# Recurrence of an RWKV-7 / SGU trunk: where three kinds of tiles lie

## The chip, the cores and the metric

The kernel runs on one core of a Trainium2 chip. A core has a matrix engine (TensorE, PE in the profile), a vector engine (DVE), a scalar engine (ACT), a general engine (POOL) and a sync engine (SP) that issues DMAs. Each engine works through its own list of instructions in order; waits between engines are semaphores. The metric is the device time of one execution in microseconds (us), the median over the runs.

## The reference

Two layers over one sequence of 512 tokens of width 1024. Layer 0 is RWKV-7 time mixing, layer 1 a spatial gating unit (SGU); each is followed by a SwiGLU feed-forward block (FFN), and every sub-layer stands between two RMS norms. The change lies in layer 0, whose core is, for each of 16 heads of 64 features:

```python
xx = _token_shift(x) - x
xs = x[None] + xx[None] * mix[:, None, None, :]
r, k, v = jnp.einsum('cbtd,cde->cbte', xs[:3], w_rkv)
...
S = (S * w_t[:, :, None, :]
     + sa[..., None] * b_t[:, :, None, :]
     + v_t[..., None] * k_t[:, :, None, :])
y = jnp.einsum('bhij,bhj->bhi', S, r_t)
...
y = y + jnp.sum(r_h * k_h * r_k, axis=-1, keepdims=True) * v_h
return (y * g) @ w_o
```

Here sa is S times a_t. Each head's y is normalised over its 64 features before the bonus term is added.

## The kernel before

The recurrence is done in chunks of 64 tokens, 8 chunks, for four batches of four heads (b = 0 to 3). The list PLAN fixes the order in which the stages are written: P (r and k projections), E (decay and key features, early stage), X0 (the inputs of the value projection), V0 to V3 (value projection), F (front: within-chunk matrices), B (back: inverts the 64-step triangular systems and builds each chunk's transition), S (the scan over chunks), N (group norm, bonus, gate). After N3 comes the output projection with w_o, then FFN 0, the SGU layer and FFN 1. The list is not the order of execution: a scheduler takes all instructions of all five engines and puts them in order by priorities and by when it expects a tile's buffer to be free. So which pool a tile lives in decides which instruction has to wait for which earlier tile, and that moves instructions on every engine.

The steps that the prediction speaks of, by name and line:

- X0: `mixed_split` makes eight tiles `xsp`, one for each block kt of 128 features. Each is made from `xs` by ACT (L612) and DVE (L613), then split in a high part (ACT cast, L179) and a low part (DVE, L180). The value projection `v_proj` multiplies them, twelve matmuls for each kt, kt 0 first, so a late `xsp` stops the PE. String XV names the pool of each: x for the residual's pool, e for the early stage's, s for the general slots.
- E3, the last early stage, shares the engines with X0: `ssp` (PE, L785), its Relu (ACT, L787), a table load and logarithm (L788), a table load and exponential (L789).
- F: groups of four matmuls `lm` (L851), copied by ACT into `MV`, `LA` and `BX`, masked by POOL; transposes `bkt` (L865). `BX` holds, for each half of the chunks and of the heads, what later extends the matrices (`gh`, L966).
- B: DVE transposes `LA` into `LX` (L882), inverts in 15 steps of two operations (`tm` L896, `Dm` L898), transposes the result twice (`hn` L901, `Dt` L902). PE and DVE then pass `Qp`, `Qs` (L921), `Np`, `Tp`, `Q2p`, `T2p`, `mp` and eight `gh` to each other, and DVE adds each `gh` into `MV` (L968, L969).
- S: for each chunk `us` (PE, L995), `su` (DVE, L997), `Yp` (PE); the result is copied into `Y` by ACT (L1010).
- N: `mu` (L1024), centring (L1026), variance `va` (L1030), a root by Newton steps (L214 to L223), `vt` transposes of the bonus (L1045, after `hn`, L1042, and before ACT's `ob`, L1047), `yt` (L1070, L1071), gate (L1074, L1075).

The pools: the residual's pool xp has 4 buffers of 128 x 1024 floats and is idle in the recurrence, apart from the tiles that borrow it; the early stage's pool, tag e2, has E2 = 7; the general slots, tag s, 17. Helpers `s4`, `xslot` and `e2` take a tile from the general slots, the residual's pool and the early stage's pool. `front` also takes its `ST` and `LA`, and `back` its `LX`, from e2.

Of the kernel before, what the change touches and what calls it, by code (L numbers as in the profile page):

```python
# [7 lines left out]
F32 = mybir.dt.float32  # L8
# [5 lines left out]
P = 128  # L14
# [3 lines left out]
TT = T // P  # L18
H2 = 8
C = 64  # L20
# [12 lines left out]
SLOTS = 17  # L33
E2 = 7
PLAN = "P0 E0 P1 E1 P2 E2 P3 E3 X0 F0 B0 F1 V0 V1 V2 V3 B1 S0 F2 S1 F3 N0 B2 N1 B3 S2 N2 S3 N3".split()
XV = "xxxessss"
XSLOTS = 13
LAG = 2
PLAIN = 2
# [91 lines left out]
class Trunk:  # L131
# [384 lines left out]
    def rwkv(self, x0):  # L516
# [3 lines left out]
        with ExitStack() as ctx:  # L520
# [14 lines left out]
            def e2(name, shape=(P, 2, T), dt=F32):  # L535
                return rp.tile(list(shape), dt, name=name, tag="e2", bufs=E2)

            def s4(name, shape, dt=F32):
                return self.slot(shape, dt, name)

            def xslot(name, shape, dt=F32):
                return self.xp.tile(shape, dt, name=name, tag="x", bufs=TT)
# [73 lines left out]
            def mixed_split(c, where):  # L616
                r = []
                for kt in range(KT):
                    t = mixed(c, kt)
                    new = dict(x=xslot, s=s4, e=e2)[where[kt]]  # L620
                    s = new("xsp", [P, 2, T], F32R)
                    self.split(s[:, 0, :], s[:, 1, :], t)
                    r.append(s)
                return r
# [192 lines left out]
            def upper(t, base):  # L817

                g.affine_select(out=t, in_=t, compare_op=ALU.is_ge, fill=0.0, base=base, pattern=[[0, 4], [1, C]],
                                channel_multiplier=-1)  # L820
# [3 lines left out]
            def front(b, o):  # L824

                MV, ST, BX = {}, {}, {}
# [14 lines left out]
                for hh, q in units:  # L841
                    st, mv = ST[hh][:, q], MV[hh, q]

                    bx = BX[hh, q] = s4("BX", [P, 4, 4, C])
                    for hd in range(2):
                        g.tensor_copy(bx[head[hd], 2 + hd], self.ident[head[hd], head[hd]].unsqueeze(1).broadcast_to([64, 4, C]))
                    for hd in range(2):
                        rows, other = head[hd], head[1 - hd]
                        lm = self.bank("pl", "lm")
                        for cc in range(4):  # L850
                            mm(lm[:, cc * P:(cc + 1) * P], st[:, cc].rearrange("p n t -> p (n t)"), mv[:, cc, :, hd, :], start=True, stop=True)  # L851
                        lv = lm.rearrange("p (c a t) -> p c a t", c=4, a=2)
                        la = LA[:, q, 4 * hh:4 * hh + 4]
                        a.copy(mv[other, :, :, hd], lv[other])
                        for n in range(2):
                            upper(mv[other, :, n, hd], n - 1)
                        a.copy(la[rows], lv[rows, :, 0, :])
                        upper(la[rows], -1)
                        a.copy(bx[rows, 1], lv[rows, :, 1, :])
                        upper(bx[rows, 1], 0)  # L860

                    sf = st.rearrange("p c n t -> p c (n t)")
                    pt = self.bank("pl", "bkt")
                    for cc in range(4):
                        nc.tensor.transpose(pt[:, cc * P:(cc + 1) * P], sf[:, cc], self.ident)  # L865
                    pv = pt.rearrange("p (c h f) -> p c h f", c=4, h=2)
                    for hd in range(2):
                        rows, other = head[hd], head[1 - hd]
                        a.copy(bx[rows, 0], pv[rows, :, hd])
                        a.copy(bx[other, 2 + hd], pv[other, :, hd])  # L870
# [100 lines left out]
            def scan(b, o, then=None):  # L971

                MV, pc = o["MV"], o["pc"]
                Y = xslot("Y", [P, TT, 2, P])

                def new_su(c):
                    su = rp.tile([P, 2, 2, C], F32, name="su", tag="su", bufs=4)
# [8 lines left out]
                for c in range(NC):  # L986
                    hh, cc = c // 4, c % 4
# [21 lines left out]
                    if par == 1:  # L1009
                        a.copy(Y[:, tt].rearrange("p q f -> p (q f)"), yp[:, 0:2 * P])  # L1010
                    if c < NC - 1:
                        su = nsu
                    if then and c == NC // 2 - 1:
                        then(Y)
                return Y

            def group_norm(Y, tts):

                n, n4 = len(tts), 4 * len(tts)
                ts = slice(tts[0], tts[-1] + 1)  # L1020
                y4 = Y[:, ts].rearrange("p t q (h v) -> p (t q h) v", h=2)
                yf = Y[:, ts].rearrange("p t q f -> p (t q f)")
                mu = self.sm.tile([P, n4], F32, name="mu", tag="mu", bufs=2)
# [71 lines left out]
            xr, kr, ops, Y = None, {}, {}, {}  # L1095
            for n in PLAN:
                f, b = n[0], int(n[1])
# [6 lines left out]
                elif f == "X":  # L1104
                    xs = mixed_split(2, XV)
                elif f == "V":
# [164 lines left out]
```

## Time and profile before

| | |
|---|---|
| time, median of 3 runs | 1363.42 us (1361.05 to 1363.58) |
| profiled execution | 1364.19 us, span 1362.5 us |
| mean granted PE clock | 0.975 |
| PE busy | 1289.8 us, 95% of the span, 9812 matmuls |
| DVE busy | 894.2 us, 66% |
| ACT busy | 694.9 us, 51% |
| POOL busy | 193.2 us, 14% |

Times below are in us from the start of the span. In the tables of stretches each engine has its busy time and its number of instructions, and PEclk is the clock granted to the PE as a share of full speed. In the lists of waits, an engine and line is followed by what it waited for, the total, how often and the longest. In the timelines a row has start, duration, engine, line, operation, and in brackets the idle time before it and what ended that.

Three stretches of the recurrence matter here: the value projection, 172 to 252, with the fronts F0 and F1 and the back B0 around it; the scans and backs, 252 to 401; and the end of the recurrence with the output projection, up to 473.

### The profile page before, as it was taken

The numbers are of one execution on the slowest core, as the hardware profiler recorded it, in microseconds if no ns is written. First come the engines' busy times: TensorE is split into PE (matmuls) and PEld (weight loads), VectorE is DVE, ScalarE is ACT, GpSimd is POOL, SyncE is SP. The second block draws the span as 40 slices with busy tenths as digits, with TensorE's granted clock in tenths as the row PEclk, the third lists the DMA queues.
The fourth block names the chain that finished last, engine by engine and source line by source line (L and its number), as shares of the span: only waits on it lengthen the run. The fifth ranks groups of instructions, "written<-read, shape, count | busy, mean of one in ns | idle before, by whom it ended". The sixth has DMA issues, their size and how long they took to land. (4 is left out here: it accounts for less than half of the span.)

```text
span 1362.5 us, 24563 instructions
## 1 busy us (share of the span) xinstructions
PE 1289.8 (95%) x9812; PEld 1120.0 (82%) x9812; DVE 894.2 (66%) x1515; ACT 694.9 (51%) x1240; POOL 193.2 (14%) x311
## 2 busy tenths in 40 slices
PE   5989999989789989999999999999989999999998
PEld 3657789878677787999998887878878999998886
DVE  7875676477837499778785325575479787786223
ACT  7975795576333364455454314543364554464221
POOL 1000184575100024000000002010122000000000
PEclk9989999899799988999999999999989999999999
DMA  5136595322214233343323232242322433323321
GB/s 157 38 89 154 138 221 162 108 73 78 78 42 153 63 105 90 112 117 100 106 78 109 93 116 86 79 151 80 108 82 72 126 109 94 109 63 117 99 94 62
DMA packets 217266, 140.10 MB, mean 103 GB/s; under 512 B 67856, under 2 KB 193344, under 8 KB 217152
## 3 DMA queue, kind: packets, MB, share of 16 engines
q1 hardware_dynamic: 215856, 133.81, 34.0%
q0 software_dynamic: 1296, 4.72, 1.0%
q8 instruction: 77, 1.26, 0.4%
q14 instruction: 37, 0.30, 0.1%
HBM read 124.35 MB, written 14.16 MB: 102 GB/s over the span
## 5 line engine op out<-in xcount | busy, mean ns | idle before, releaser
L180 DVE TENSOR_TENSOR wlo<-wraw,whi 128x1024 fp32r<-128x1024 f32 x105 | 129.6, 1234 | 195.2 <-ACT whi L179 187.4
L179 ACT CAST whi<-wraw 128x1024 fp32r<-128x1024 f32 x105 | 110.0, 1048 | 227.9 <-PE acc L204 136.5
L204 PE MATMUL acc<-whi,actw 128*128 128x512 f32 x704 | 220.7, 394 | 0.0
L204 PEld LDWEIGHTS acc<-whi,actw 128*128 128x128 f32 x704 | 132.3, 188 | 30.6
L204 PE MATMUL Q<-bc,whi 128*128 128x256 f32 x864 | 156.3, 281 | 1.1 <-ACT hn L421 1.1
L204 PE MATMUL acc<-wlo,actw 128*128 128x512 f32 x352 | 138.7, 394 | 0.0
L204 PEld LDWEIGHTS Q<-bc,whi 128*128 128x128 f32 x864 | 133.4, 189 | 1.5 <-ACT hn L421 1.3
L179 ACT CAST whi<-wsum 128x1024 fp32r<-128x1024 f32 x72 | 75.5, 1051 | 101.1 <-DVE wsum L377 35.5
L204 PE MATMUL Q<-bc,wlo 128*128 128x256 f32 x432 | 121.5, 281 | 0.0
L204 PE MATMUL Z<-bc,whi 128*128 128x256 f32 x576 | 107.9, 285 | 3.3 <-ACT whi L179 3.3
L204 PE MATMUL R<-bc,whi 128*128 128x256 f32 x576 | 108.1, 285 | 0.9 <-ACT Q L392 0.9
L180 DVE TENSOR_TENSOR wlo<-wsum,whi 128x1024 fp32r<-128x1024 f32 x72 | 86.7, 1221 | 18.9 <-ACT whi L179 18.9
L204 PE MATMUL gu<-hT,whi 128*128 128x256 f32 (+1 forms) x384 | 92.2, 334 | 3.6 <-DVE hT L62 3.4
L204 PEld LDWEIGHTS Z<-bc,whi 128*128 128x128 f32 x576 | 90.6, 192 | 4.2 <-ACT whi L179 4.2
L204 PEld LDWEIGHTS R<-bc,whi 128*128 128x128 f32 x576 | 91.0, 192 | 1.3 <-ACT Q L392 1.1
L204 PE MATMUL proj<-xsp,whi 128*128 128x512 f32 x256 | 85.2, 411 | 5.7 <-ACT xsp L179 3.1
L179 ACT CAST whi<-wq 128x1024 fp32r<-128x1024 f32 x54 | 56.7, 1049 | 58.1 <-issue 18.4
L180 DVE TENSOR_TENSOR wlo<-wq,whi 128x1024 fp32r<-128x1024 f32 x54 | 65.9, 1222 | 30.9 <-ACT whi L179 30.8
L204 PE MATMUL Z<-bc,wlo 128*128 128x256 f32 x288 | 81.9, 284 | 0.0
L204 PE MATMUL R<-bc,wlo 128*128 128x256 f32 x288 | 81.9, 284 | 0.0
L204 PEld LDWEIGHTS Q<-bc,wlo 128*128 128x128 f32 x432 | 81.9, 189 | 0.0
L204 PEld LDWEIGHTS acc<-wlo,actw 128*128 128x128 f32 x352 | 66.1, 188 | 15.3
(346 smaller groups left out, 2883.3 us busy)
## 6 DMA issues: line engine op xcount, KB each, us to landing
wraw<-in_ffn_w_down_dram SPq DMA_DIRECT2D x44, 512.0 KB, 3.7
wq<-in_ffn_w_gate_dram SPq DMA_DIRECT2D x72, 256.0 KB, 3.0
wq<-in_ffn_w_up_dram SPq DMA_DIRECT2D x72, 256.0 KB, 3.5
wraw<-in_rwkv_w_rkv_dram SPq DMA_DIRECT2D x24, 512.0 KB, 4.9
wraw<-in_sgu_w_in_dram SPq DMA_DIRECT2D x16, 512.0 KB, 4.2
x<-in_x_dram SPq DMA_DIRECT2D x8, 512.0 KB, 4.2
ST<-sb SPq DMA_DIRECT2D x8, 512.0 KB, 6.2
MV<-sa SPq DMA_DIRECT2D x32, 128.0 KB, 3.8
```

What stands on the lines that cost most here:

```text
L179: self.nc.scalar.copy(hi, src)
L180: self.nc.vector.tensor_tensor(lo, src, hi.bitcast(F32), op=ALU.subtract)
L204: self.nc.tensor.matmul(out, l, r, start=start, stop=stop, skip_group_check=resumed)
```

## The change

Three places take their tiles elsewhere. The eight inputs of the value projection came from the residual's pool (kt 0 to 2), e2 (kt 3) and the general slots (kt 4 to 7); now kt 0 and 1 come from e2 and the other six from the general slots. The `BX` tiles of the even batches (F0 and F2, four tiles each) came from the general slots and now come from the residual's pool. The scan's result `Y` came from the residual's pool and now comes from e2. No size of a pool changes and no arithmetic.

```diff
-XV = "xxxessss"
+XV = "eessssss"
...
-                    bx = BX[hh, q] = s4("BX", [P, 4, 4, C])
+                    bx = BX[hh, q] = (s4 if b % 2 else xslot)("BX", [P, 4, 4, C], F32)
...
-                Y = xslot("Y", [P, TT, 2, P])
+                Y = e2("Y", (P, TT, 2, P))
```

All five engines' lists come out in another order. Two places carry the prediction. The first is ACT at the start of the value projection, where the last tiles `xsp` are cast while E3 finishes. Before:

```order
L179 CAST xsp<-xs 128x512
L772 ACTIVATE cum<-cum,lnh 128x1024
L787 ACTIVATE tws<-ssp,tiny 128x512
L179 CAST xsp<-xs 128x512
L777 ACTIVATE kp<-tws,hka 128x512
L787 ACTIVATE tws<-ssp,tiny 128x512
L179 CAST whi<-wraw 128x1024
L788 ACT_TABLE_LOAD
L788 ACTIVATE tws<-tws,tiny 128x1024
```

And after:

```order
L772 ACTIVATE cum<-cum,lnh 128x1024
L787 ACTIVATE tws<-ssp,tiny 128x512 x2
L612 ACTIVATE xs<-h,omix 128x512
L179 CAST xsp<-xs 128x512
L788 ACT_TABLE_LOAD
L788 ACTIVATE tws<-tws,tiny 128x1024
L179 CAST xsp<-xs 128x512
L789 ACT_TABLE_LOAD
```

Before, both casts (kt 6 and kt 7) stood ahead of the second Relu of E3 (L787). Now the cast for kt 6 stands behind both Relus and behind the making of kt 7's `xs`, and the cast for kt 7 behind the table load and the logarithm as well. On the PE the two `ssp` products that the Relus read moved in the same way: before, 18 and 27 value products stood behind the first and the second; now both stand together behind 60 value products, with 34 of the 36 products with kt 5, 6 and 7 right behind them.

The second place is DVE at the third inversion (batch 2), around `LX`. Before:

```order
L222 SCALAR_TENSOR_TENSOR nr_t<-nr_t,nr_a 128x16
L882 STREAM_TRANSPOSE LX<-LA 128x1024
L223 SCALAR_TENSOR_TENSOR nr_y<-nr_t,nr_y 128x16
L896 TENSOR_TENSOR tm<-LX,Dm 128x2x15
L221 TENSOR_TENSOR nr_t<-nr_y 128x16
L898 TENSOR_TENSOR Dm<-Dm,tm 128x2x15
L222 SCALAR_TENSOR_TENSOR nr_t<-nr_t,nr_a 128x16
L896 TENSOR_TENSOR tm<-LX,Dm 128x2x28
L223 SCALAR_TENSOR_TENSOR nr_y<-nr_t,nr_y 128x16
L968 TENSOR_TENSOR MV<-gh,BX 128x4x64
```

And after:

```order
L968 TENSOR_TENSOR MV<-gh,BX 128x4x64
L969 TENSOR_TENSOR MV<-gh,MV 128x4x64
L1075 TENSOR_TENSOR ob<-gate,ob 128x512
L997 TENSOR_TENSOR su<-us,pc 64x2x64
L1071 SCALAR_TENSOR_TENSOR ob<-yt,vecT_101,ob 128x512
L997 TENSOR_TENSOR su<-us,pc 64x2x64
L882 STREAM_TRANSPOSE LX<-LA 128x1024
L896 TENSOR_TENSOR tm<-LX,Dm 128x2x15
L898 TENSOR_TENSOR Dm<-Dm,tm 128x2x15
L1075 TENSOR_TENSOR ob<-gate,ob 128x512
```

Before, `LX` of batch 2 stood inside the Newton steps of N0, ahead of the first of batch 1's eight pairs of additions into `MV` (L968, L969). Now it stands behind the last of these pairs and behind four of the seven `su` of scan S1.

The third place is DVE at the end of that inversion. Before, batch 2's `Qs` (L921) and the fourth inversion's `LX` stood thus:

```order
L902 STREAM_TRANSPOSE Dt<-Dm 128x32x32
L997 TENSOR_TENSOR su<-us,pc 64x2x64
L180 TENSOR_TENSOR g2l<-g_4827,g2h 128x256
L997 TENSOR_TENSOR su<-us,pc 64x2x64 x2
L921 TENSOR_TENSOR Qs<-Qp,id_144 128x512
L1024 TENSOR_REDUCE mu<-Y 128x16
L882 STREAM_TRANSPOSE LX<-LA 128x1024
L180 TENSOR_TENSOR wlo<-wraw,whi 128x1024
L1025 TENSOR_SCALAR mu<-mu 128x16
L896 TENSOR_TENSOR tm<-LX,Dm 128x2x15
L1026 TENSOR_TENSOR Y<-Y,mu 128x1024
```

And after:

```order
L1026 TENSOR_TENSOR Y<-Y,mu 128x1024
L898 TENSOR_TENSOR Dm<-Dm,tm 128x2x15
L901 STREAM_TRANSPOSE hn<-Dm 128x32x32
L902 STREAM_TRANSPOSE Dt<-Dm 128x32x32
L882 STREAM_TRANSPOSE LX<-LA 128x1024
L1030 TENSOR_REDUCE va<-hn 128x16
L896 TENSOR_TENSOR tm<-LX,Dm 128x2x15
L214 TENSOR_SCALAR nr_a<-va 128x16
L898 TENSOR_TENSOR Dm<-Dm,tm 128x2x15
L216 TENSOR_SCALAR nr_h<-nr_a 128x16
L921 TENSOR_TENSOR Qs<-Qp,id_144 128x512
```

The mean and the centring of N1 (L1024 to L1026), which stood behind `Qs`, now stand ahead of the transposes of batch 2's inverse; `LX` of batch 3 and N1's variance (L1030) stand ahead of `Qs`. Three low splits of w_o's weights (`wlo`, L180), which stood between `Qs` and batch 3's transposes, have left this stretch for a place behind batch 3's inversion.

Three more moves matter. On the PE, all of F1's `lm` and `bkt` and B0's first `mp` now stand ahead of the last value product (before, two `lm` groups and two `bkt` of F1 and that `mp` stood behind it). Between the end of S1 and batch 2's first `gh` the PE's list now holds F3's last four `lm` and two `bkt` and the steps of B2, and little else. At the end, the first half of N3 (`vt`, `yt`, gate) stands inside S3, before behind its last `Yp`.

## The prediction

> **What bounds the kernel now.** I read the page first, for the busiest engine and for where it is not busy.
>
> ```profile
> PE 1289.8 (95%) x9812; PEld 1120.0 (82%) x9812; DVE 894.2 (66%) x1515; ACT 694.9 (51%) x1240; POOL 193.2 (14%) x311
> PE   5989999989789989999999999999989999999998
> ```
>
> The PE is the bound of the program as a whole. A slice of the second row is 34 us: from the 17th on (545 us, FFN 0 and later) it is a row of nines. What follows the recurrence is thus a solid chain of PE work that the change leaves alone, and a microsecond gained or lost before it reaches the end undiminished. So only the recurrence counts. I took it in stretches of 20 us; the PE has its busy time behind the stretch's length, and PEclk follows behind POOL.
>
> ```profile
> 180.00:200.00 20.00, 17.41 (x171) 16.91 (x169) 14.15 (x13) 17.89 (x34) 14.53 (x20) 1.00 0.98 212
> 340.00:360.00 20.00, 12.59 (x241) 10.40 (x240) 17.91 (x53) 9.38 (x14) 4.52 (x8) 0.70 0.25 80
> 440.00:460.00 20.00, 17.73 (x75) 13.86 (x76) 7.79 (x18) 3.93 (x7) 0.00 (x0) 0.91 0.33 103
> 460.00:480.00 20.00, 16.03 (x80) 12.36 (x79) 12.99 (x43) 11.96 (x35) 3.37 (x2) 1.00 0.27 80
> ```
>
> The value projection (180 to 200) is nearly full. The worst stretch is 340 to 360, where the PE idles 7.4 us and DVE is busy 17.91 of 20: there DVE's inversion of batch 3 is the bound. The end (440 to 480) idles 2.27 + 3.97 = 6.2 us. The lists of the PE's waits say what ended the idle time, first for 165 to 255, then 252 to 400, then 400 to 500.
>
> ```profile
> PE lm L851 <- DMA MV<-sa: 1.5, 1, 1.5
> PE lm L851 <- POOL MV L819: 1.1, 1, 1.1
> ...
> PE vt L1045 <- DVE hn L1042: 3.8, 1, 3.8
> ...
> PE vt L1045 <- ACT ob L1047: 1.3, 1, 1.3
> PE yt L1070 <- ACT ob L1047: 0.8, 1, 0.8
> ```
>
> No wait is for a buffer in so many words: a pool shows itself in which instruction stands where. So I go by the order of the lists, and price what moved with rows of the trace.
>
> **Part one: the inputs of the value projection.** On the PE, the value products run at a fixed pace, and the two `ssp` come among them. ACT and DVE rows of the same moment stand below.
>
> ```profile
> 177.23 1.02 PE L785 MATMUL ssp<-tws,bones 128*128 128x512 f32 x2
> 179.03 0.40 PE L204 MATMUL v<-whi,xsp 128*128 128x256 f32 x2
> 180.80 0.40 PE L204 MATMUL v<-whi,xsp 128*128 128x256 f32 x2
> ...
> 176.23 0.71 ACT L612 ACTIVATE xs<-h,omix 128x512 f32<-128x512 f32 x1
> 179.86 0.61 ACT L179 CAST xsp<-xs 128x512 fp32r<-128x512 f32 x1
> 181.08 0.68 ACT L787 ACTIVATE tws<-ssp,tiny 128x512 f32<-128x512 f32 x1
> 182.71 1.28 ACT L788 ACT_TABLE_LOAD   x1
> 184.00 1.15 ACT L788 ACTIVATE tws<-tws,tiny 128x1024 f32<-128x1024 f32 x1
> ...
> 180.50 0.69 DVE L180 TENSOR_TENSOR xsp<-xs,xsp 128x512 fp32r<-128x512 f32 x1 [1.43 <-ACT xsp L179]
> ```
>
> Between the two value rows lie 15 products in 1.77 us, 0.118 each. Before, the last `xsp` was split by 180.50 + 0.69 = 181.2, well ahead of its use. With the change, 60 products stand ahead of both `ssp`. If they begin near 172.4, the `ssp` begin at 172.4 + 60 x 0.118 = 179.5 and end at 180.5. The two Relus (0.68 each) then end near 181.6, kt 7's `xs` (0.71) at 182.3, the cast for kt 6 (0.61) at 182.9, the table load at 184.2, the logarithm at 185.3, the cast for kt 7 at 185.9, and its split (0.69) at 186.6. The PE has worked through kt 5 and 6 (24 products, 2.8 us) at 183.4 at the earliest. It waits for kt 7 until 186.6: 3.2 us of new idle time, split over kt 6 and kt 7. In return, the two waits for `MV` in the list above (1.5 and 1.1) fall away, since the DMA and POOL work they wait for lands while the PE stands: net **+0.6**. Bounds: 0, if ACT reaches the Relus earlier, since kt 7 then arrives earlier too; +4.9, if the 2.6 are not won back and the PE restarts at a lower clock. That last has a row: in 340 to 360, where the 3.8 us wait lies, the granted clock was 0.70; the lost 0.30 on the next 48 products (5.7 us) is 1.7.
>
> [...]
>
> **Part two: `BX` in the residual's pool, F1 and F3.** The general slots that F0's `BX` no longer holds go to F1, whose last two `lm` groups and `bkt` come ahead of the end of the value projection. That is work moved on a full PE, not removed: S0 begins later by that work, and has that much less of it between its own steps. I take **0**. Bounds: it could win the 1.1 us of the second wait quoted above, if that copy is the one that now comes early, or lose as much, if the longer stretch before S0 is not made up behind it.
>
> **Part three: the two inversions on DVE.** This is the largest move. Rows of DVE, before:
>
> ```profile
> 301.10 1.96 DVE L882 STREAM_TRANSPOSE LX<-LA 128x1024 f32<-128x1024 f32 x1
> 304.13 0.42 DVE L968 TENSOR_TENSOR MV<-gh,BX 128x256 f32<-128x256 f32 x1
> 317.23 0.41 DVE L969 TENSOR_TENSOR MV<-gh,MV 128x256 f32<-128x256 f32 x1
> 324.68 1.92 DVE L902 STREAM_TRANSPOSE Dt<-Dm 128x1024 f32<-128x1024 f32 x1
> 334.53 0.69 DVE L921 TENSOR_TENSOR Qs<-Qp,id 128x512 f32<-128x512 f32 x1 [0.16 <-PE Qp L918]
> 366.68 0.38 DVE L968 TENSOR_TENSOR MV<-gh,BX 128x256 f32<-128x256 f32 x1
> ...
> L898 DVE TENSOR_TENSOR Dm<-Dm,tm 128x30 f32<-128x30 f32 (+7 forms) x30 | 8.2, 274 | 0.4
> L896 DVE TENSOR_TENSOR tm<-LX,Dm 128x30 f32<-128x30 f32 (+7 forms) x30 | 8.1, 269 | 0.4
> L180 DVE TENSOR_TENSOR wlo<-wraw,whi 128x1024 fp32r<-128x1024 f32 x3 | 3.6, 1208 | 0.9 <-ACT whi L179 0.9
> L1026 DVE TENSOR_TENSOR Y<-Y,mu 128x1024 f32<-128x1024 f32 x1 | 1.2, 1224 | 0.0
> L1024 DVE TENSOR_REDUCE mu<-Y 128x16 f32<-128x1024 f32 x1 | 1.2, 1220 | 1.3 <-ACT Y L1010 1.3
> L1025 DVE TENSOR_SCALAR mu<-mu 128x16 f32<-128x16 f32 x1 | 0.5, 474 | 0.0
> L1075 DVE TENSOR_TENSOR ob<-gate,ob 128x512 f32<-128x512 f32 x3 | 2.1, 692 | 1.0 <-PE gate L1074 0.9
> ```
>
> (The lower rows are groups over 298 to 367; both inversions lie in it, so one has half of 8.2 + 8.1.)
>
> The additions of batch 1 come first now: without `LX` and the first steps ahead they may begin some 2.7 us earlier, 301.4, and run at their pace of before (304.13 to 317.64, 13.5 us) to 314.9; with 0.6 from part one, 315.5. One `ob` (0.7) later `LX` of batch 2 starts, near 316.5, where it had started at 301.10. It ends at 318.5. The 30 operations take 8.2 us. Among them now stand an `ob` and two splits of `oT` of its size (2.1 together), mean, scaling and centring of N1 (1.2 + 0.5 + 1.2), and three `su` and two small weight pieces that I put at 2: 7 in all. The last `su` also has to wait for the scan, which I put at 2 more. That makes 318.5 + 8.2 + 7 + 2 = 335.7, two transposes like `Dt` (1.92 each) 339.5, `LX` of batch 3 (as the other, 1.96), the variance (a reduction of the mean's size, 1.2) and small steps (1) 343.7, so near 344 for `Qs`, against 334.53: **nine us later**.
>
> From `Qs` to the first addition of batch 2 it took 366.68 - 334.53 = 32.15 before, DVE busy in most of it. Of what DVE did there, these are now done elsewhere: `LX` 1.96, mean 1.2, its scaling 0.5 and the 1.3 of waiting ahead of it, centring 1.2, variance 1.2, three `wlo` 3.6: 11.0. That leaves 21.2, so the additions start at 344 + 21.2 = 365.2. Against 366.68 that is **-1.4**: nearly all that `LX` lost, the shorter list behind `Qs` gives back. Bounds: -3.4 if the `su` do not hold DVE up; +2.5 if both inversions run 2 us slower, with more waits.
>
> The PE needs time for the same chain, so I checked it: in batch 3, `Qs` to the first `gh` (L966) took
>
> ```profile
> 381.33 0.68 DVE L921 TENSOR_TENSOR Qs<-Qp,id 128x512 f32<-128x512 f32 x1
> 400.88 1.37 PE L966 MATMUL gh<-BX,MVt 64*128 64x128 f32 x13
> ```
>
> 19.6 us, with scan work between. From 344 that is 363.6, before DVE's 365.2; DVE still decides. From there on, batch 3's own chain repeats the same steps, shifted.
>
> **Part four: `Y` in e2, and the end.** With half of N3's transposes inside S3, the waits for `ob` in the third list (1.3 + 0.8) are covered by the scan's chain. Behind the last `Yp` there are then fewer transposes and about as many output products, so what `ob` no longer delays may wait for the second half's `ob` instead. I take half of the 2.1, **-1.1**; bounds -2.1, all of it, and +1, if the moved transposes hold up S3's own steps by about one of the waits quoted.
>
> **The sum**: +0.6 is already within the 315.5 and so in the -1.4; 0 - 1.4 - 1.1 = -2.5. The profiled execution took 1364.19, the median is 1363.42, 0.8 lower. From the median: 1363.4 - 2.5 = **1360.9**, 1361 us. About 0.2%, 2.7 us, is what a measurement here can tell from no change, so my forecast lies just inside that. All the lower bounds together are -3.4 - 1.1 - 2.1 = -6.6, all the upper ones, without the +4.9 that has a case of its own, 2.5 + 1.1 + 1 = +4.6: its own range is 1357 to 1368.
>
> **Rivals.** *First, the late inputs pass through:* the PE stops at kt 7, F0's `lm` and `LA` stand behind it, and batch 0's chain and S0 move by all of it. For it: the PE is nearly full to 252, so nothing ahead absorbs a stop. Against: 2.6 us of other waits lie just behind. It decides once the stop exceeds those 2.6; the whole stop and the clock's 1.7 make +4.9: about 1368. *Second, the hole grows:* between S1's end and batch 2's `gh` the PE has little left but B2's own steps, and waits for each `Qs`, `bdT` and `Q2p` in turn at a clock of 0.70 or below; DVE in turn waits for the slowed PE. It decides if the PE's answers, not DVE's list, end the chain. The stretch 340 to 360 lost 0.30 of the clock on 12.6 us of busy PE, 3.8 us; with as much once more, part three at its upper bound of +2.5 and the end at -1.1 it is +5.2: about 1368. [...] *Third, the holes close:* against my part three the two chains run beside each other, and the 7.4 us that the PE idles in 340 to 360 go, and the end's 2.1 whole: -9.5, about 1354. For it: three `wlo` and a mean leave DVE's fullest stretch. Against: `LX` of batch 2 starts 15 us later.
>
> **How the numbers follow.** Forecast 0.45 (of it 0.15 faster, 0.27 the same, 0.03 slower), the late inputs 0.18, the hole 0.11, closed holes 0.26 (nearly all faster). Faster 0.15 + 0.25 = 0.40; same 0.27 and 0.01 = 0.28; slower 0.32. The range that leaves out two in ten: 1352 to 1370.
>
> **What would show it.** Part one: a PE wait at `v` for ACT or DVE `xsp` near 183, about 3 us, and the `lm` waits for `MV` gone. Part three: `LX` of batch 2 near 316, `Qs` near 344, the first addition of batch 2 near 365, batch 3's first `gh` near 399. Part four: no PE wait for `ob` behind the last `Yp`, and the first `ptr` of the residual near 471 to 472. Wrong it is if batch 2's additions start beyond 368 or before 361, or if the end of the recurrence shifts by more than they do.

## The result: 1.1% slower

The changed kernel takes 1377.77 us, the median of 9 runs (1370.61 to 1383.38), against 1363.34 us for the kernel before in runs beside it (9 runs, 1356.99 to 1369.98). The ratio is 1.011, with a 95% interval from 1.0086 to 1.0134: about 14 us slower, where 2.5 us faster was forecast. The profiled execution took 1374.99 us, span 1373.3, 10.8 longer than the one before. Every trace here is one execution: over the nine of the changed kernel the mean granted clock went from 0.960 to 0.973, and over those of the kernel before that ran beside the later experiments from 0.966 to 0.978, so what a single trace says of the clock is good to some microseconds only.

The page after, with the rows that answer to those of before:

```profile
span 1373.3 us, 24558 instructions
PE 1294.1 (94%) x9812; PEld 1124.8 (82%) x9812; DVE 900.0 (66%) x1515; ACT 694.2 (51%) x1240; POOL 190.1 (14%) x311
PE   6989989988889989999999999999989999999998
```

The work is the same, 9812 products. In the row of slices (34 us each) eights stand where nines stood from 172 to 206 and from 309 to 343 us, and an eight where the seven stood from 343 to 377; from 560 on both rows are alike. The stretch 160 to 560 tells more. First before, then after:

```profile
160.00:560.00 400.00, 364.28 (x4335) 319.17 (x4334) 279.23 (x582) 221.69 (x480) 144.67 (x253) 0.94 0.39 109
```

```profile
160.00:560.00 400.00, 358.47 (x4222) 312.20 (x4221) 274.03 (x572) 217.39 (x475) 137.69 (x245) 0.92 0.37 105
```

The PE is idle for 35.7 us of it before and for 41.5 after, and the clock is lower. A PE at half clock looks as busy as any other, so a table of busy times hides this loss: after, the PE is busy for all of 370 to 375 at 0.50, and eight `mp` take 2.08 us at 0.50 (from 366.60) where eight take 1.16 at 1.00 (from 378.27). I price it as busy time times (1 - clock), stretch by stretch of 20 us from 160 to 560, and add the idle time. Before that is 35.7 + 18.5 = 54.2 us, after 41.5 + 26.9 = 68.4: 14.2 more, and 8.4 of them are clock. In the rest of the span (0 to 160, and 560 to the end) the same sum is 46.1 before and 45.3 after. So the loss lies in the recurrence, and in these two traces its larger part is not waiting but slow work. The sum is bookkeeping: both kernels do the same products, so whatever time is lost must show as idle time or as slow work. It says where the time went, not why.

Where it arises is seen on DVE and in the queue of SP. Of before, three rows that the forecast did not show, from the timelines of SP, DVE and PE (batch 3's loads, batch 2's last addition, the scan's last step):

```profile
275.50 1.25 SPq L829 DMA_DIRECT2D ST<-sb  x2
...
378.16 0.41 DVE L968 TENSOR_TENSOR MV<-gh,BX 128x256 f32<-128x256 f32 x1
...
431.21 0.68 PE L1008 MATMUL Yp<-su,MV 128*64 128x64 f32 x8
```

And after, rows of the same three timelines in the order of time:

```profile
305.29 0.42 DVE L968 TENSOR_TENSOR MV<-gh,BX 128x256 f32<-128x256 f32 x1
...
320.14 1.26 SPq L829 DMA_DIRECT2D ST<-sb  x2
...
320.27 0.41 DVE L969 TENSOR_TENSOR MV<-gh,MV 128x256 f32<-128x256 f32 x1
...
323.84 1.89 DVE L882 STREAM_TRANSPOSE LX<-LA 128x1024 f32<-128x1024 f32 x1
...
325.28 2.05 PE L851 MATMUL lm<-MV,ST 128*128 128x128 f32 x16 [1.98 <-DMA ST<-sb]
...
328.31 0.69 DVE L1075 TENSOR_TENSOR ob<-gate,ob 128x512 f32<-128x512 f32 x1 [2.10 <-PE gate L1074]
...
352.57 0.69 DVE L921 TENSOR_TENSOR Qs<-Qp,id 128x512 f32<-128x512 f32 x1
...
372.42 0.42 DVE L968 TENSOR_TENSOR MV<-gh,BX 128x256 f32<-128x256 f32 x1 [0.35 <-PE gh L966]
...
389.98 0.42 DVE L968 TENSOR_TENSOR MV<-gh,BX 128x256 f32<-128x256 f32 x1
...
411.54 1.71 PE L966 MATMUL gh<-BX,MVt 64*128 64x128 f32 x16 [0.68 <-ACT MVt L961]
...
456.18 0.33 PE L1008 MATMUL Yp<-su,MV 128*64 128x64 f32 x2
...
487.33 0.60 PE L267 MATMUL ptr<-ident,x 128*128 128x128 f32 x4
```

The two `ST` loads of batch 3 are issued at 320.14 where they were issued at 275.50. The PE reaches batch 3's first `lm` before they land, waits 1.98 us, and N0's gate and the scan's next step stand behind that `lm` in its list; DVE then waits 2.10 for that gate in the middle of the inversion. Batch 2's additions start at 372.42, 5.7 later than before. From the first of them to the last takes 17.6 us, where it took 11.5. Batch 3's first `gh` is 10.7 late, and the residual's first `ptr` 13.9 (487.33 against 473.45).

The clock explains a part of the 17.6. Stretches of 5 us of the kernel before, and then of the changed kernel:

```profile
345.00:350.00 5.00, 1.71 (x8) 1.72 (x9) 4.11 (x13) 2.58 (x4) 0.00 (x0) 0.79 0.30 103
350.00:355.00 5.00, 2.80 (x48) 2.07 (x48) 4.88 (x21) 3.11 (x5) 0.00 (x0) 0.50 0.05 20
355.00:360.00 5.00, 4.65 (x47) 3.99 (x44) 4.06 (x12) 1.16 (x2) 0.00 (x0) 0.50 0.01 3
360.00:365.00 5.00, 4.71 (x33) 3.69 (x32) 4.23 (x7) 0.59 (x2) 0.00 (x0) 0.85 0.27 91
```

```profile
345.00:350.00 5.00, 3.54 (x129) 2.65 (x128) 4.97 (x4) 4.30 (x11) 1.94 (x6) 0.97 0.02 5
350.00:355.00 5.00, 3.61 (x168) 3.02 (x172) 4.97 (x19) 1.27 (x3) 3.05 (x8) 1.00 0.33 105
355.00:360.00 5.00, 2.75 (x137) 2.59 (x124) 4.68 (x16) 1.38 (x4) 0.00 (x0) 0.55 0.03 7
360.00:365.00 5.00, 4.22 (x74) 3.43 (x74) 4.57 (x14) 2.73 (x5) 0.00 (x0) 0.50 0.01 3
365.00:370.00 5.00, 4.11 (x16) 3.17 (x14) 4.77 (x10) 0.86 (x2) 0.00 (x0) 0.50 0.00 0
370.00:375.00 5.00, 5.00 (x25) 4.47 (x25) 3.58 (x6) 0.00 (x0) 0.00 (x0) 0.50 0.19 58
375.00:380.00 5.00, 5.00 (x42) 4.37 (x41) 2.17 (x5) 2.16 (x4) 0.00 (x0) 0.90 0.34 103
```

From 355.5 to 376.0 the PE runs at half clock. Before, the half clock lay from 348 to 361.5 and ended five us ahead of the additions, in time that DVE's inversion mostly needed anyway. After, it lies under the first `mp` and `gh`, which DVE waits for, and under the first 3.6 us of the additions. From the first to the last of batch 2's additions (372.42 to 389.98) the PE is busy for 16.90 us at a mean clock of 0.90, where it was busy for 11.00 us at 1.00. So 1.7 of the 6.1 us are clock; most of the rest is work that has moved in, among it two groups of `mp` that stood ahead of the first addition before.

### The profile page after: what moved, and what is told of

It is laid out like the page before. It is cut to its first block, busy times and chain, and to the rows that moved or that the text cites. A ratio compares the mean times of both kernels' runs of the same rounds, so it can differ in the third digit from the quotient of the medians.

```text
span 1373.3 us, 24558 instructions
## 1 busy us (share of the span) xinstructions
PE 1294.1 (94%) x9812; PEld 1124.8 (82%) x9812; DVE 900.0 (66%) x1515; ACT 694.2 (51%) x1240; POOL 190.1 (14%) x311
## 5 line engine op out<-in xcount | busy, mean ns | idle before, releaser
L180 DVE TENSOR_TENSOR wlo<-wraw,whi 128x1024 fp32r<-128x1024 f32 x105 | 129.2, 1231 | 182.5 <-ACT whi L179 178.9
L180 DVE TENSOR_TENSOR wlo<-wsum,whi 128x1024 fp32r<-128x1024 f32 x72 | 86.7, 1221 | 18.9 <-ACT whi L179 18.9
L180 DVE TENSOR_TENSOR wlo<-wq,whi 128x1024 fp32r<-128x1024 f32 x54 | 65.9, 1222 | 32.1 <-ACT whi L179 32.1
L179 ACT CAST whi<-wq 128x1024 fp32r<-128x1024 f32 x54 | 56.7, 1050 | 58.5 <-issue 18.5
L204 PEld LDWEIGHTS acc<-wlo,actw 128*128 128x128 f32 x352 | 66.1, 188 | 15.2
```

Of the source, the lines that this page charges most:

```text
L179: self.nc.scalar.copy(hi, src)
L180: self.nc.vector.tensor_tensor(lo, src, hi.bitcast(F32), op=ALU.subtract)
L204: self.nc.tensor.matmul(out, l, r, start=start, stop=stop, skip_group_check=resumed)
```

## Experiments: one part at a time

Each of the three parts was put into the kernel before alone and in pairs. The edits are the lines of the change, so one line stands for each here. The inputs alone:

```diff
-XV = "xxxessss"
+XV = "eessssss"
```

> Only the inputs of the value projection move (two in the early stage's pool, six in the general slots); the extension matrices and the scan's results stay where they were. Theory A (the scan's results in the early stage's pool hold back the loads of batch 3's ST, and with them the third inversion): -3 to +3 us against the kernel before; the third LX starts at 301 to 312, the ST loads of batch 3 are issued before 295. Theory B (the late inputs of the value projection pass through to the end): +3 to +8 us, with 3 us of waits for xsp on the PE near 183 and every later step shifted by that. Theory C (the loss is time at half PE clock): the time goes with the mean granted clock, 0.975 for no change, 0.970 for +10.

Ratio 1.0076 (1.006 to 1.0093), 10 us slower. `LX` of batch 2 starts at 312.76, and batch 2's additions at 365.44, 1.2 us earlier than before. The PE idles even less than before in 160 to 560 (31.8 us against 35.7); in this trace all of the loss is clock, 32.8 against 18.5. So theory A does not account for this, and B fails too, since batch 2's additions are not later. C's account fits: the median of the mean granted clocks is 0.971 over its five executions, 0.975 over those of the kernel before beside them.

The extension matrices alone:

```diff
-                    bx = BX[hh, q] = s4("BX", [P, 4, 4, C])
+                    bx = BX[hh, q] = (s4 if b % 2 else xslot)("BX", [P, 4, 4, C], F32)
```

> Only the extension matrices of the even batches move to the residual's pool. Theory A: the third LX stands behind all of batch 1's additions here as well, but batch 3's ST is loaded earlier than in the changed kernel, so half of the loss at most: 0 to +7 us; the third LX at 312 to 320. Theory B: no late inputs, so -3 to +2. Theory C: as the clock shows; a slower time only with a mean clock under 0.973.

Ratio 1.0331 (1.0307 to 1.0356), 45 us slower, outside every expectation. Rows of its PE and DVE timelines say why: batch 0's front stops half way.

```profile
193.13 1.05 PE L851 MATMUL lm<-MV,ST 128*128 128x128 f32 x8
...
224.53 0.60 PE L865 MATMUL bkt<-ident,ST 128*128 128x128 f32 x4
...
238.88 1.96 DVE L882 STREAM_TRANSPOSE LX<-LA 128x1024 f32<-128x1024 f32 x1 [2.73 <-POOL LA L819]
```

Between 193 and 224 neither `lm` nor `bkt` runs, and the first `LX` starts at 238.88 in place of 213.23. The front needs four `BX` tiles from four buffers, of which the value projection's inputs hold three until the projection is through with them. That is theory D below: the parts are not three independent edits.

The scan's results alone:

```diff
-                Y = xslot("Y", [P, TT, 2, P])
+                Y = e2("Y", (P, TT, 2, P))
```

> Only the scan's results move to the early stage's pool. Theory A: most of the loss of the changed kernel, +8 to +14 us; ST of batch 3 issued after 310, the PE waits about 2 us at an lm for that load, the third LX after 318. Theory B: no loss, -3 to +3, since the inputs of the value projection are as before. Theory C: slower only with longer stretches at half clock between 340 and 430.

Ratio 1.0142 (1.0123 to 1.016), 19 us slower, more than the three parts together and more than A's 8 to 14. The third `LX` starts at 322.46 and batch 3's loads go out at 319.26, as A expected, and the loss is mostly idle time: 50.6 us of it, with a clock loss of 21.4.

Inputs and extension matrices without the scan's results:

> The change without its third part: inputs and extension matrices move, the scan's results stay. Theory A: the loss falls to what the extension matrices alone cost, 0 to +7 us. Theory B: +3 to +8, about that of the inputs alone. Theory C: time with the clock, as above.

Ratio 1.011 (1.009 to 1.013), the changed kernel's own, and more than A or B allowed. With the inputs moved away, the 45 us of the extension matrices are gone. But the third `LX` starts at 324.16 here too, although batch 3's loads are out by 281 (SP's timeline: 279.14 and 280.38): neither `Y` in the early stage's pool nor late loads are needed to make it late. There the scan's results share the residual's four buffers with four `BX`; that this is what delays it was not tried by itself.

The two pairs that were left:

> Extension matrices and scan results move, the inputs of the value projection stay, three of them in the residual's pool. Theory D (the parts hang together: batch 0's four BX tiles need the residual's four buffers, so three of them wait until the value projection is done with its inputs there): the first LX near 239 as in the run with the extension matrices alone (213 before), +30 to +50 us. If D is wrong and each part has its own price: 44 + 19 less what the changed kernel shows, +5 to +20, with the first LX near 216.

Ratio 1.0254 (1.0195 to 1.0313). The first `LX` starts at 238.85, exactly where it stood with the extension matrices alone. D holds.

> The change without its second part: inputs and scan results move, the extension matrices stay in the general slots. Theory D: no tile waits for the residual's pool, so no such loss; what the scan's results cost in the early stage's pool stays, +8 to +18. If the extension matrices in the residual's pool are what costs the changed kernel its 14: -2 to +5.

Ratio 1.0153 (1.0106 to 1.0199), 21 us, a little above D's 8 to 18. So it is not the extension matrices that cost the changed kernel its 14 us: without them it is no faster.

Taken together: inputs +0.8%, scan's results +1.4%, both +1.5%; adding the extension matrices to both gives +1.1%. No part is free, and none is the whole cause. The bookkeeping comes out for all of them, each profile's idle PE time plus clock loss from 160 to 560, against its own execution's time:

| profile | idle | clock loss | more than before | own time, more than before's 1364.2 |
|---|---|---|---|---|
| before | 35.7 | 18.5 | | |
| the change | 41.5 | 26.9 | 14.2 | 10.8 |
| inputs | 31.8 | 32.8 | 10.4 | 7.2 |
| extension matrices | 56.2 | 33.2 | 35.2 | 39.6 |
| scan's results | 50.6 | 21.4 | 17.8 | 14.3 |
| inputs, matrices | 41.6 | 27.8 | 15.2 | 13.2 |
| matrices, results | 47.6 | 43.8 | 37.2 | 40.4 |
| inputs, results | 44.8 | 32.8 | 23.4 | 25.3 |

The two right columns agree within 4.4 us in each row.

## Experiments: the control, the loads and the pool

Does any new order lose? The control moves one tile that the change does not need to move:

```diff
-XV = "xxxessss"
+XV = "xxxsssss"
```

> A control: the kernel before with one tile moved, the value projection's input kt 3, from the early stage's pool to a general slot; nothing of the change is in it. Theory A and B, each tied to a part of the change: -3 to +3. The form of C that any new order loses (the kernel before has the one order that its numbers were chosen for): +5 to +15, with more idle PE time and clock loss before 560 than the 54 us of the kernel before.

Ratio 1.0003 (0.9983 to 1.0023): the same, although its PE list differs from the one before in about as many places as the change's. So a new order need not cost anything, and the sharper form of C, that any new order loses, falls; one order of this kind was tried. Its trace also shows how far one execution can be off: it was the slowest of eleven (1369.56 us, median 1365.60), with 60.3 us of idle time and clock loss against 54.2.

Next, the late loads. Batch 3's two `ST` tiles come from the general slots, all else as in the change:

```diff
-                    st = ST[hh] = e2("ST", (P, 2, 4, 2, C))
+                    st = ST[hh] = (s4 if b == 3 else e2)("ST", (P, 2, 4, 2, C), F32)
```

> The changed kernel with batch 3's two ST tiles in general slots, so that their loads need not wait for an early-stage tile that the scan's results hold. Theory A: the loads are issued before 310, the PE's wait of 2 us at lm goes, the third LX starts by 318 in place of 323.8, and the time is +4 to +9 against the kernel before. Theory C: the time goes with idle plus clock loss before 560, wherever ST lies; +8 to +16 if these do not shrink.

Ratio 1.007 (1.0046 to 1.0093). What A says of the loads and of DVE came out, as rows of its SP and DVE timelines show:

```profile
293.63 0.54 SPq L829 DMA_DIRECT2D ST<-sb  x1
...
315.49 1.94 DVE L882 STREAM_TRANSPOSE LX<-LA 128x1024 f32<-128x1024 f32 x1
...
363.47 0.42 DVE L968 TENSOR_TENSOR MV<-gh,BX 128x256 f32<-128x256 f32 x1
```

The last load is out at 293.63, the third `LX` starts at 315.49, and batch 2's additions at 363.47, 3.2 us earlier than in the kernel before. So the early-stage pool did hold the loads back, and taking `ST` elsewhere was worth 9 us at that place (372.42 to 363.47). Not all of it is the loads: in this run's DVE list `LX` stands ahead of the last two pairs of batch 1's additions, and N1's mean and centring have left the inversion. Its time lies just above A's 4 to 9 us. Yet the kernel is still some 9.5 us slower than before: nothing of the 3.2 arrives. The stretch 340 to 480 in the tables by stretches, of before, and then of this kernel with four of its stretches of 5 us:

```profile
340.00:480.00 140.00, 119.92 (x1395) 96.74 (x1394) 88.31 (x232) 54.46 (x123) 9.04 (x13) 0.93 0.28 87
```

```profile
340.00:480.00 140.00, 120.02 (x1472) 98.84 (x1472) 86.11 (x220) 48.96 (x107) 4.58 (x11) 0.84 0.26 81
...
345.00:350.00 5.00, 4.20 (x186) 4.00 (x176) 4.76 (x17) 2.10 (x3) 0.00 (x0) 0.50 0.03 7
350.00:355.00 5.00, 1.31 (x25) 0.78 (x25) 4.88 (x19) 2.32 (x4) 0.00 (x0) 0.50 0.00 0
355.00:360.00 5.00, 3.93 (x62) 3.46 (x58) 4.66 (x12) 1.26 (x2) 0.00 (x0) 0.50 0.01 3
360.00:365.00 5.00, 5.00 (x26) 4.45 (x26) 4.58 (x7) 0.59 (x1) 0.00 (x0) 0.50 0.00 0
```

The PE is busy for as long in both, and the clock is 0.84 against 0.93. Priced in stretches of 5 us, the clock takes 17.8 us of this stretch, where it took 7.8. In this trace the remaining loss of this kernel is clock.

A pool with one more buffer, and one general slot less:

```diff
-SLOTS = 17
-E2 = 7
+SLOTS = 16
+E2 = 8
```

> The changed kernel with eight buffers in the early stage's pool and sixteen general slots (7 and 17 before). Theory A: the scan's results have a buffer of their own, so +0 to +6. Theory C, in the form that any new order of the lists loses: +8 to +18.

Ratio 1.0084 (1.0058 to 1.0109). The third `LX` starts at 318.78, between the change and the kernel with `ST` in slots; batch 3's loads go out at 315.43, hardly earlier than at 320.14. One more buffer, at the price of a general slot, is not enough to bring them forward, and A's 0 to 6 us is missed.

Last, on top of `ST` in slots, the scan's results of odd batches went back to the residual's pool:

```diff
-                Y = e2("Y", (P, TT, 2, P))
+                Y = (xslot if b % 2 else e2)("Y", (P, TT, 2, P))
```

> The changed kernel with batch 3's ST in general slots and the scan's results of the odd batches back in the residual's pool. If what is left of the loss in the ST run comes from Y in the early stage's pool: -2 to +4. If it comes from the clock alone, which no pool sets: +5 to +12, and the time goes with idle plus clock loss in 160 to 560 (54 us in the kernel before).

Ratio 1.0059 (1.0033 to 1.0084), not to be told from the run with `ST` in slots alone. The 8 us lie in the range that was given for the clock, and `Y` has no further part that shows.

## Experiments: filling the PE

Can the clock be held up? Useless products were added to batches 2 and 3, into a PSUM tile that nothing reads. First in the changed kernel, behind `Tp`, `Q2p` and `T2p`, two each:

```diff
+            def warm(b, src):
+                if b in WARM:
+                    pt = self.bank("pl", "warm")
+                    for _ in range(NWARM):
+                        mm(pt, self.ident, src.rearrange("p u s -> p (u s)"), start=True, stop=True)
...
+                warm(b, Qs)
                 Dn2 = el("Dn2", (P, 16, 32))
```

> The changed kernel with 18 useless products (128x128x512, about 0.5 us each at full clock) on the PE in batches 2 and 3 (and their order around it), six in each of the two between Tp and the bdT copies, where the PE waits for ACT and DVE. Theory C (half of the loss is PE time at half clock, because the PE's small steps and waits let the clock fall): the clock in 355 to 425 rises, and in spite of some 6 us of added work the time is +6 to +12 against the kernel before, less than the changed kernel's +14.4. Theory A (late loads of ST and the longer chain alone) or B: no gain; the added work shows, +15 to +21.

That text counts wrongly: it is twelve products in all, six in each batch. And each stands in the trace as two matmuls, of 0.46 us at full clock (eight from 406.22 to 409.85), so 11 us of work were added and not 6. Ratio 1.0091 (1.0056 to 1.0126): with 11 us more to do, some 2 us less than the change, though the intervals overlap. Idle time plus clock loss fell from 68.4 to 61.8; the mean granted clock of its five executions is 0.974 to 0.979, where the change's nine had 0.960 to 0.973. That speaks for C, but the time alone would not show it.

The same filling in the kernel before:

> The kernel before with twelve useless products (128x128x512) between Tp and the bdT copies, six in batch 2 and six in batch 3, some 6 us of added PE work. Theory C: the granted clock in 345 to 362 rises from 0.5, that in 390 to 395 from 0.72; but DVE's inversion of batch 3 ends the stretch 340 to 366 anyway, so little is won there: -2 to +5. If the PE is the bound in both places and the clock has no part: +6 to +8.

Ratio 1.0043 (1.0017 to 1.007), 6 us for 11 us of work. Half of the fill was hidden or won back; the expectation has the same miscount. And with half of it (one product in place of two) in the kernel with `ST` in slots:

> The changed kernel with batch 3's ST in general slots, and with three useless products in batch 2 and three in batch 3 (half of the earlier filling, some 3 us). Theories A and C together, if their shares add up: +9.5 for the ST run, less 2 to 5 of clock: +3 to +8 against the kernel before. If the order decides in a way that neither names: +9 to +18.

Ratio 1.0068 (1.0043 to 1.0093), unchanged from 1.007, for 5.5 us more work: at the edge of the second range, above the first.

Then the fill was set among the small products themselves. `Qp`, `Np`, `Tp` and `Q2p` are runs of 32 to 128 products of 32x32, and in each run a product of 128x128 by 256 columns was put after every 32 small ones or so, twelve for each of the two batches (`Qp` is the product of `Dn` and `LA`, so its fill reads `Dn`; the others read `Qs`):

```diff
+                def warm(u, every, src):
+                    if b in WARM and u % every == every - 1:
+                        mm(wt[:, 0:256], self.ident, src, start=True, stop=True)
...
                 for u in range(16):
+                    warm(u, 4, qf)
                     for z, hd, x in quarters:
                         mm(Tp[z:z + 32, u * 32:(u + 1) * 32], Qs[z:z + 32, u, :], Dt[z:z + 32, u, x, :], start=True, stop=True)
```

> The changed kernel with batch 3's ST in general slots, and in batches 2 and 3 twelve useless products each (128x128x256, about 0.27 us) set among the small 32x32 products of Qp, Np, Tp and Q2p: 6.5 us of added PE work. The ST run without them has as much idle PE time in 340 to 480 as the kernel before (20.0 us) but 17.8 us lost to the clock against 7.8. Theory E (the 32x32 products do not count as work for the clock, so it falls while the PE is at them): the half-clock stretches of 345 to 367 and 390 to 395 shrink, idle plus loss falls by 6 or more, and the time is +4 to +10. Theory F (the clock falls with the idle time alone): no less loss, and +13 to +18.

Ratio 1.0099 (1.0075 to 1.0122): 4 us slower than without the fill, which is F's range. But a filled product takes 0.63 us in its two matmuls (383.82 to 384.45), so 24 of them are 15 us of work, and some 11 us were won back. The rows of 5 us show the clock at 1.00 right through the small products:

```profile
345.00:350.00 5.00, 5.00 (x171) 3.22 (x170) 4.87 (x19) 1.48 (x3) 0.00 (x0) 1.00 0.02 7
385.00:390.00 5.00, 5.00 (x100) 3.55 (x100) 0.88 (x2) 0.88 (x3) 0.00 (x0) 1.00 0.33 114
390.00:395.00 5.00, 5.00 (x109) 3.34 (x111) 0.00 (x0) 0.77 (x2) 0.00 (x0) 1.00 0.06 13
```

Without the fill, 345 to 350 stood at 0.50 and so did 390 to 395. The same in the kernel before, in batch 3 alone:

> The kernel before with the twelve small useless products (3.3 us) in batch 3 alone, where the clock falls to half at 390 to 395; the order of scan S2 and of what lies behind it changes with them. Theory E: the clock in 385 to 400 stays at 1, which wins some 2 to 3 us at full price: -2 to +4. Theory F: +3 to +7.

Ratio 1.0032 (1.001 to 1.0054), 4.4 us for 7.6 us of work, again in F's range. The clock in 385 to 400 went up as expected, to 0.84 and then 1.00, but 365 to 385, ahead of it, stood at 0.5 to 0.6 in this profile, where it had been at 1.00.

What was won was eaten by the price of the fill, so the last three runs made it cheap. The products read the upper halves of the same float32 numbers as bfloat16, and the trace then has 24 matmuls for the 24 products, where it had 48:

```diff
-                        mm(wt[:, 0:256], self.ident, src, start=True, stop=True)
+                        half = lambda t: t.bitcast(mybir.dt.bfloat16).rearrange("p (n two) -> p n two", two=2)[:, :, 1]
+                        mm(wt[:, 0:256], half(self.ident), half(src), start=True, stop=True)
```

> As the run with small steps filled in batches 2 and 3 of the ST kernel, but the 24 useless products read the upper halves of the same values as bfloat16 numbers, one pass in place of several. In that run 24 float32 products cost some 16 us (two passes each, about 0.35 us a pass) and won back nearly as much. Theory E, with the fill at a third of the price or less: +0 to +6 us, against +9.5 without any and +13.5 with the dear fill; the half-clock stretches at 345 to 367 and 390 to 395 shrink as there. Theory F: the time falls only by the price, to +9 or so, and those stretches are back.

Each takes 0.22 us now (392.52 to 392.74 in the rows below), 5 us in all. Ratio 1.0025 (1.0003 to 1.0047), 3.4 us slower than before, where the same kernel without the fill was 9.5 slower (1.0046 to 1.0093) and the change 14 (1.0086 to 1.0134). 9.5 - 3.4 + 5 = 11 us won back, as with the dear fill, and E's 0 to 6 us is met.

```profile
340.00:480.00 140.00, 126.38 (x1583) 101.03 (x1569) 87.33 (x221) 51.01 (x109) 5.16 (x12) 0.91 0.28 83
...
350.00:355.00 5.00, 5.00 (x143) 3.71 (x143) 5.00 (x25) 0.15 (x1) 0.00 (x0) 0.50 0.01 3
...
392.52 0.29 PE L920 MATMUL warm<-Qs,ident 128*128 128x256 bf16 x1
392.74 0.69 PE L936 MATMUL Np<-Qs,Dt 32*32 32x32 f32 x32
...
PE Tp L940 <- issue: 0.4, 1, 0.4
```

And the waits of the kernel with `ST` in slots, for the same 340 to 480, without the fill:

```profile
PE Tp L930 <- issue: 3.3, 2, 2.5
...
PE Np L927 <- issue: 1.0, 1, 1.0
```

The fill did two things: the clock in 340 to 480 rose from 0.84 to 0.91, and the waits inside the runs of small products in which the PE waited for nothing but its next instruction shrank from 4.3 us to 0.4. But the half-clock stretch of batch 2, which E had shrinking, is hardly shorter (348.0 to 368.5, against 343.9 to 367.8), although the PE is busy without a break from 350 to 355 in it; what went is the one from 390 to 395. E (the small products let the clock fall) and F (only idle time does) are not told apart by this, since those waits are idle time too, and went with the fill.

> The kernel before with the same cheap fill in batches 2 and 3 (part of batch 2's falls in one piece, behind twelve products of Tp). Theory E: idle plus clock loss in 160 to 560, 54 us before, falls by more than the fill costs: -6 to 0. If any new order of scan S2 loses more than the clock gives: +2 to +8.

Ratio 1.0025 (1.0003 to 1.0046). That is the second range: in the kernel before the fill wins nothing net; in 340 to 480 its clock loss is 7.6 us against 7.8.

> The ST kernel with the scan's results of the odd batches back in the residual's pool (+8 us as it was) and the cheap fill in batches 2 and 3. Theory E: -3 to +4. Theory F: +6 to +11.

Ratio 1.0073 (1.0049 to 1.0097): within the range that F named. In this kernel the fill won back no more than its price: idle time plus clock loss is 58.3 against 56.7 without it, each from one trace. So the fill is no rule; that it depends on where the holes lie is likely, and not shown. No kernel here beat the one before.

## Why the prediction was wrong

**What was right.** The reading of the bound: behind 560 no more was lost, and nearly all that was lost in the recurrence arrived at the end. A matmul near 600 starts 12.4 us later than the same one before, and one behind 910 starts 10.6 to 10.9 later; between lies a stay of the kernel before at half clock (850 to 855 at 0.70) that the changed one's trace does not have. Part one was right in its mechanism and nearly to the tenth (the changed kernel's ACT and DVE timelines, and its PE waits from 165 to 255):

```profile
182.08 0.63 ACT L179 CAST xsp<-xs 128x512 fp32r<-128x512 f32 x1
...
185.08 0.60 ACT L179 CAST xsp<-xs 128x512 fp32r<-128x512 f32 x1
...
185.71 0.69 DVE L180 TENSOR_TENSOR xsp<-xs,xsp 128x512 fp32r<-128x512 f32 x1 [2.12 <-ACT xsp L179]
...
PE v L204 <- ACT xsp L179: 3.0, 2, 2.1
```

The split was forecast to end at 186.6 and the PE to stop for 3.2 us in two pieces; it ended at 186.4, and the stop was 3.3 with the 0.3 it waited for DVE. The waits for `MV` went, as said, and the clock stayed at 1.00 in 180 to 200. The +0.6 took a full clock through the stop for granted, which no run shows as a rule: in the trace of the cheap fill in the `ST` kernel, with a stop of 2.7 us at the same place, it was 0.91 in 180 to 200. S0's first `us` came 1.7 us later than before (259.38 against 257.64) and batch 1's first addition 1.2 (305.29 against 304.13), so the whole stop did not pass through, and the first rival is refuted.

Part two was put at 0. Those two numbers do not contradict it, but it has no price of its own: adding the extension matrices to the inputs cost 5 us, and adding them to inputs and results cost nothing that shows.

**The step that failed: part three, up to `Qs`.** It put the third `LX` at 316.5 and batch 2's `Qs` at 344; they came at 323.84 and 352.57. Three of its terms were wrong. Batch 1's additions were put at 301.4, as if only DVE's list had held them up; the PE's first `gh` came at 303.58, and its steps for N0 and S1 stood between the pairs, so the eighth pair ended at 320.7 and not at 315.5. From there to `LX` the forecast had one `ob` (0.7); two `ob` and two `su` stood there, with waits for the PE between them, 3.1 us. And the inversion, put at 17.2 us with its interleaved work, took 19.4 (325.76 to the start of the transposes at 345.12), with the 2.10 of waiting for a gate that stood behind an `lm` that stood behind a DMA. I had followed DVE's list and the PE's, but not SP's: in SP's timeline 16 `su` loads go out ahead of batch 3's two `ST` loads before, and 28 after. These late loads account for the 2.10; the first two terms, 7.3 us together, were late before the PE waited for them. The experiment with `ST` in the general slots shows what the pool is worth, not that the lateness of the loads is the cause: there the additions start at 363.47, near the 365.2 of the forecast, but the eighth pair of batch 1 still ends late, at 319.5, and `LX` starts at 315.49 only because it stands ahead of the last two pairs. That it is near the forecast's 316.5 is luck.

The second half of part three, from `Qs` to the first addition, was put at 21.2 and took 19.9 (352.57 to 372.42). That term came out near, with DVE busy for 18.5 us of it, as it was meant.

**The step that was missing: the clock behind it.** Batch 2's additions took 6.1 us longer than before, of which 1.7 is clock, and batch 3's 3.8 longer (16.8 against 13.0), of which 3.1 is clock (the PE is busy for 15.57 us of it at 0.80). Over 160 to 560 the clock takes 8.4 us more than before. I had this as my second rival, with 0.11 and +5; the clock fell where it said, but the sum of the forecast had no term for it at all. "From there on, batch 3's own chain repeats the same steps, shifted" was the sentence that left it out. In the kernel with `ST` in slots, where the idle PE time in 340 to 480 is that of before, the clock alone keeps 10 us.

**Part four.** The first `ptr` came at 487.33, not near 472. From the last `Yp` to it the PE needed 31.1 us where it had needed 42.2, since N3's first half and more output products lay ahead; but the last `Yp` itself came 25 us later. The waits for `ob` (2.1 before) fell to 0.9 (two waits of 0.5 and 0.4), about as I took it, and it did not matter.

**The third rival** (the holes close) is refuted: the PE's idle time in 340 to 480 fell only by 4.0 (140 less 119.92, and less 123.94), and the clock took 10.0 more there (17.8 against 7.8).

So the forecast failed in the order up to `Qs` and in having no term for the clock. Why the changed order costs just this much clock stays open: orders that idle the PE less lost more of it (the inputs alone), and the clock's part differs between executions of one kernel.

## What to carry to other kernels

When tiles move between pools under a scheduler, follow the loads in the DMA queue's list as well as the engines' lists: a load that had moved behind the release of a tile stopped the PE for 1.98 us here, and DVE, which needed a product behind the stopped one, for 2.10. Price a chain of short dependent PE steps in idle time plus busy time times (1 - clock), never in busy time alone: this sum, over the recurrence, gave where the time of seven kernels went to within 4.4 us, though not why. And parts of such a change that share a pool are one change: one of them alone was 45 us slower, and 5 us slower once another had freed its buffers.

## What was not expected of the hardware

The clock fell although no wait in the 10 us before was longer than 1.4 us; the row of a low clock that the forecast went by, 0.70 in 340 to 360 of the kernel before, lies beside a wait of 3.8 us. In the changed kernel the PE was busy for 3.54 and 3.61 us of two stretches of 5 (345 to 355), and was at half clock (0.50) from 355.5 on:

```profile
353.31 1.16 PE L927 MATMUL Np<-Qs,Dt 32*32 32x32 f32 x61 [1.39 <-DVE Qs L921]
...
357.82 0.31 PE L930 MATMUL Tp<-Dt,Qs 32*32 32x32 f32 x3 [2.25 <-issue]
```

What ran in 345 to 355 were 24 products of 128x128 and runs of 32x32, 128 of them and fewer, and between the last of those, just as the clock had fallen, the PE waited 2.25 us for its next instruction, with nothing in the profile that it waited for. The return took long as well: in the kernel with `ST` in slots the PE was busy for all of 360 to 365 at 0.50, and in the changed kernel it was busy without a break from 366.6 to the return at 376.0. This stay at half clock lasted 20.5 us (355.5 to 376.0), the one before it 3.4 (341.9 to 345.3). So in this trace the clock fell over a stretch that was 70% busy by the profile, with short waits and small products in it, and returned only after 9.4 busy us. Why it stayed so long is not shown, and whether the small products let it fall stays open, as said above.
